# Four early product tiles instead of two at the start of three feed-forward stages

## The chip, the cores and the metric

The kernel runs on one core of a Trainium2 chip. The metric is the device time of one execution in microseconds (us), the median of three runs. TensorE (PE) multiplies matrices, VectorE (DVE), ScalarE (ACT) and GpSimd (POOL) work element by element, and SyncE (SP) issues the DMA transfers. Each engine takes its instructions strictly in the order of its own queue; semaphores tie the queues together. TensorE's clock has two levels here, 2.4 and 1.2 GHz; the profile gives the granted clock as a share of the upper one.

## The reference

Two layers work on 512 tokens (256 context, 256 latent; 1024 features). Each layer is a modulated feed-forward half-step, a token mixer of four parallel head groups, and a second feed-forward half-step:

```
def modulate(x, shift, scale): return x * (1 + scale) + shift
def swiglu(x, wi, wo):
    g, u = jnp.split(x @ wi, 2, axis=-1)
    return (jax.nn.silu(g) * u) @ wo

sc, scc = jax.nn.silu(c), jax.nn.silu(c_ctx)
for l in range(DEPTH):
    mod  = (sc  @ w_mod[l] + b_mod[l]).reshape(b, N_MOD, 1, d)     # latent stream
    modc = (scc @ w_mod[l] + b_mod[l]).reshape(1, N_MOD, 1, d)     # context stream
    h = h + 0.5 * mod[:, 2] * swiglu(modulate(rms_norm(h, ffn1_norm[l]), mod[:, 0], mod[:, 1]), ffn1_wi[l], ffn1_wo[l])
    ...                                        # the same for hc; then the mixer, and the second half-step
```

In the last layer only the latent stream goes on after the mixer. All of it is in float32.

## The kernel before

Features lie on partitions: the state `h` is eight chunks of 128 features by 512 tokens. A product of float32 quality is made of three products in float32r: weight and activation are each split into a high part (a cast) and a low part (the rest), and a tile of 128 output features takes 24 matmuls (`mm3`: eight hi·hi, eight hi·lo, eight lo·hi). `load_split` fetches one weight tile of 128x1024 by DMA (`raw`, three buffers), casts it on ACT (`hi`, two buffers) and subtracts on POOL or DVE in turn (`lo`, two buffers), or on the engine that it is told.

A feed-forward stage (`ffn`) makes 44 tiles `gu` (22 pairs of gate and up), two halves of 11 pairs, each followed by eight output tiles `o`. There are four such stages: the first of layer 0 starts in its own way (`first_tiles`), the later three go through `Normed`. They are called here F2 (second of layer 0, starts at 721 us), F3 (first of layer 1, 1104 us) and F4 (second of layer 1, 1715 us, with 256 token columns instead of 512).

The normalized activation `x` of such a stage needs the root of the mean square over all features, so it can't exist before the last chunk of `h` is there. To bridge this, the first tiles are early: they multiply the weights with `h` times the per-feature scale (`N.pre`, tiles `X`, made by `scale` while the stage before ends), and the factor per token (`R`) and the shift are put in afterwards. `early` therefore also multiplies the same weights with the modulation's shift (`nBs`) into a PSUM bank `bias` (32 small matmuls for a tile), `shift` sums that over partitions (an ACT copy, one matmul, a DVE copy), and `evacuate` multiplies by `R` and adds. Two tiles (NE = 2) are early. In the meantime `finish` makes `R`: sums over partitions on PE (L274), a root by thirteen small DVE instructions (L277 to L284), a broadcast by PE (L287), a copy by ACT (L290). Then `x` makes the eight chunks: chunks 2, 4 and 6 (`POOLX`) begin on POOL (L300) and go on over ACT, the others take DVE (L309), ACT (L311) and DVE (L312). The next two tiles (L497, L498, L501) run chunk by chunk over `x`, and from then on tiles follow by `mm3` (L208, L209, L211).

`mod_groups` computes the remaining modulation columns on DVE beside the first stage and beside F2: each weight row block `wm` (four buffers) is multiplied with silu(c) of one stream, spread over partitions, and summed (L149). The spread vector stands in the two PSUM tiles `c0` and `c1` and is made by 16 float32 matmuls against an identity (L142). `c0` and `c1` also hold the early tiles' `bias`, the sums of `finish`, and in the first stage two product tiles and the sums of `mod_chunk`.

The order within each engine's queue is made by the scheduler of the language when the program is built, from the data dependencies and a few hand-set ones (`behind`, `together`).

Of the kernel before, what the change touches and what calls it, by code (L numbers as in the profile page):

```python
# [20 lines left out]
AF = mybir.ActivationFunctionType  # L21
# [25 lines left out]
def hybrid_block(ctx: ExitStack, tc: tile.TileContext, D, out, dump=lambda *a: None, upto=99):  # L47
# [89 lines left out]
    def mod_groups(l, b0):  # L137

        cb = phase[2]
        for s in range(2):  # L140
            for k in range(NCH):
                mm(cb[s][:, 128 * k:128 * (k + 1)], cs[:, k, s:s + 1].broadcast_to([128, 128]), ident, start=True,  # L142
                   stop=True, skip_group_check=True)
        junk = phase[0].tile([128, 1024], F32, tag="macc", name=nm("macc"), bufs=1)
        for b in range(b0, 72):
            wm = room["wm"]()
            nc.sync.dma_start(out=wm, in_=D["wmod"][l, b])
            for s in range(2):
                stt(out=junk, in0=wm, scalar=1.0, in1=cb[s], op0=ALU.mult, op1=ALU.mult, accum_out=modT[l][:, b, s:s + 1])  # L149
            if b % 8 == 7:  # L150
                m = modT[l][:, b - 7:b + 1, :]
                tt(out=m, in0=m, in1=v3(prm[l][:, P_BM + b - 7:P_BM + b + 1], 8).broadcast_to([128, 8, 2]), op=ALU.add)
            yield
# [59 lines left out]
    class Normed:  # L213
# [52 lines left out]
               op0=ALU.add, op1=ALU.mult)  # L266
            return A, self.late[c][:, 0, :]

        def finish(self, W, PS, tx, ptag):
            self.W, self.tx = W, tx  # L270
            nb = self.n // 128
            ps = PS("n", "ssq")
            for j in range(nb):
# [15 lines left out]
            self.R = kept("R")  # L289
            (nc.vector.tensor_copy if self is norms[0] else nc.scalar.copy)(self.R[:, self.wc], ps[:, self.wc])  # L290
            self.bias = PS(ptag, "bias")

        def x(self, cs_):
            for c in cs_:
# [1 line left out]
                hi, lo = self.W(self.n, s="xh", dt=F32R, tag=self.tx), self.W(self.n, s="xl", dt=F32R, tag=self.tx)  # L296
                wc = self.wc
                A, B = self.AB(c)
                if c in POOLX and not self.late:
                    nc.gpsimd.tensor_tensor(out=t, in0=h[c][:, self.off:T], in1=self.R[:, wc], op=ALU.mult)  # L300
                    for s in self.streams:
                        o = self.sl[s]
                        act(t[:, o], t[:, o], AF.Identity, scale=A[:, s:s + 1], bias=B[:, s:s + 1])
                    nc.scalar.copy(hi[:, wc], t)
                    tt(out=lo[:, wc], in0=t, in1=hi[:, wc].bitcast(F32), op=ALU.subtract)
                else:
                    for s in self.streams:
                        o, b = self.sl[s], B[:, s:s + 1]
                        stt(out=t[:, o], in0=h[c][:, 256 * s:256 * (s + 1)], scalar=A[:, s:s + 1], in1=self.R[:, o],  # L309
                            op0=ALU.mult, op1=ALU.mult)  # L310
                        act(hi[:, o], t[:, o], AF.Identity, bias=b)  # L311
                        i = stt(out=lo[:, o], in0=t[:, o], scalar=b, in1=hi[:, o].bitcast(F32), op0=ALU.add,  # L312
                                op1=ALU.subtract)
                    self.last = i
                self.xs.append((hi, lo))

        def early(self, ps, hi, lo, cc):
# [7 lines left out]
                    behind(i, self.rstd)  # L325
            for k in range(NCH):
                mm(ps[:, cc], lo[:, k, :], self.pre[k][0][:, cc], start=False, stop=(k == NCH - 1))
            b = self.bias[:, 256 * n:256 * n + 128]
            for w in (hi, lo):
                for k in range(NCH):  # L330
                    j = 32 * (k % 4)
# [3 lines left out]

        def shift(self, n):

            b = self.bias[:, 256 * n:256 * n + 128]
            t = self.W(128, s="shift")
            nc.scalar.copy(t, b)  # L340
            b = self.bias[:, 256 * n + 128:256 * n + 130]
            mm(b, t, cst[:, C_SUM:C_SUM + 2], start=True, stop=True, skip_group_check=True)
            sb = small(2, "bias", bufs=4)
            nc.vector.tensor_copy(sb, b)
            return sb
# [5 lines left out]
                op0=ALU.mult, op1=ALU.add)  # L351

    NE = 2
    XC = {2: (range(4), range(4, 8)), 3: (range(2), range(2, 5), range(5, 8))}[NE]
    POOLX = (2, 4, 6)

    def first_tiles(N, wi):
# [68 lines left out]
    def ffn(l, N, wi, wo, m0, streams, hooks={}, nxt=None, fill=None):  # L426
# [10 lines left out]
                next(fill[0], None)  # L437

        if N is not norms[0]:
            N.finish(W, PS, "x", "b")  # L440
        gate = small(16, "gate").rearrange("p (c s) -> p c s", s=2)

        def evacuate(i, gps, ups, bias):
# [20 lines left out]

        ready = []
        head = first_tiles(N, wi) if N is norms[0] else []
        NE = 0 if head else 2
        wt = lambda t: load_split(wi[l, t // 2, t % 2], 1024, nc.gpsimd if t <= NE + 1 else None)
        for half in range(2):
            av = []  # L470
            for i in range(11 * half, 11 * half + 11):
# [3 lines left out]
                for t in range(2 * i + len(gu), 2 * i + 2):  # L475
# [3 lines left out]
                    hi, lo = v3(hi, 8), v3(lo, 8)  # L479
                    if t < NE:  # L480
                        bias.append(N.early(ps, hi, lo, cc))
                        if t:
                            N.x(XC[t - 1])
                        if t == NE - 1:
                            ready.append(wt(NE))
                            N.x(XC[NE - 1])
                    elif t == NE and NE:

                        bias += [None, None]
# [49 lines left out]
    def mixer(l, need_ctx, N, nxt):  # L539
# [179 lines left out]
        for c in range(NE):  # L719
            hi, lo = [v3(a, 8) for a in wt(c)]  # L720
            ps = PS("a", "xbc")
            pend.append((c, ps, N.early(ps, hi, lo, allc)))
            if c:
                N.x(XC[c - 1])
        ready.append(tmw(0))
        N.x(XC[NE - 1])
        xs = N.xs


# [726 lines left out]
def _layout(a):  # L1456
# [5 lines left out]
    cs[:, :, 0] = a["c_ctx"].reshape(8, 128).T  # L1462
    cs[:, :, 1] = a["c"][0].reshape(8, 128).T
    r["cs"] = cs.reshape(128, 256)
    wm = a["w_mod"].reshape(L, 8, 128, 9216)
    r["wmod"] = a["w_mod"].transpose(0, 2, 1).reshape(L, 72, 128, 1024).copy()
    g = wm[0, ..., :2048].reshape(2, 4, 128, 2, 8, 128).transpose(4, 0, 2, 1, 3, 5)
# [81 lines left out]
```

## Time and profile before

| | us |
|---|---|
| median of 3 runs (lowest, highest) | 1928.61 (1928.08, 1929.88) |
| the profiled execution | 1928.47 |
| its span, first to last instruction | 1926.7 |
| TensorE busy (share of span) | 1857.7 (96%) |
| VectorE busy | 1104.3 (57%) |
| ScalarE busy | 797.4 (41%) |
| GpSimd busy | 668.4 (35%) |
| mean granted TensorE clock | 0.975 |

The span is the time from the first to the last instruction of the program; the execution's own time is 1.8 us longer. Busy shares are averages over stages of very different kinds, so what matters is the stretch where the change acts: which engine is idle there and what ended its idle time. Matmuls overlap in the records: the time between two starts is the cost, not the printed duration.

### The profile page before, as it was taken

How to read it: one execution, taken by the hardware profiler on the slowest of the kernel's cores; microseconds unless marked ns; L12 is line 12 of the kernel's file. 1: busy time of each engine (PE TensorE's matmuls, PEld its weight loads, DVE VectorE, ACT ScalarE, POOL GpSimd, SP SyncE). 2: the span in 40 equal slices, each digit the busy share in tenths (PEclk: the TensorE clock that was granted, in tenths of full speed). 3: DMA queues.
4: the chain of work that ended last, by engine and by line, in shares of the span. 5: the costliest groups of instructions: out<-in, count | busy, mean ns of one | idle time of the engine just before them, and what ended most of it. 6: DMA issues, size and time to landing. Idle time of an engine off the chain costs nothing.

```text
span 1926.7 us, 25732 instructions
## 1 busy us (share of the span) xinstructions
PE 1857.7 (96%) x9698; PEld 1500.1 (78%) x9698; DVE 1104.3 (57%) x1952; ACT 797.4 (41%) x1338; POOL 668.4 (35%) x487
## 2 busy tenths in 40 slices
PE   8999999999999998999999989999999998989999
PEld 5788888887765566888888868888888875579999
DVE  5599961368477767999971451121124966674322
ACT  3232233346557544332233442223233575655443
POOL 3233233243323213332333343323323432246564
PEclk8999999999999998999999989999999998989999
DMA  9377842324221012877752322233323332024564
GB/s 361 118 263 241 268 152 89 90 91 132 77 88 34 1 55 93 266 251 254 263 193 81 109 74 91 86 111 99 99 84 100 105 114 66 23 99 162 177 191 128
DMA packets 85244, 259.01 MB, mean 134 GB/s; under 512 B 9312, under 2 KB 15856, under 8 KB 84992
## 3 DMA queue, kind: packets, MB, share of 16 engines
q1 hardware_dynamic: 85056, 257.32, 41.5%
q8 instruction: 76, 1.25, 0.3%
q14 instruction: 48, 0.39, 0.1%
q10 hardware_dynamic: 64, 0.05, 0.0%
HBM read 256.23 MB, written 1.10 MB: 134 GB/s over the span
## 4 chain that ended last, share of the span: by engine, by line
PE 56%; DVE 5%; ACT 1%; issue 1%; POOL 0%; ACTq 0%; DVEq 0%; POOLq 0%
PE gu L208 10%; PE gu L209 10%; PE gu L211 10%; PE o L208 5%; PE o L209 5%; PE o L211 5%; DVE x L309 1%; PE wo L208 1%; PE gu L498 0%; PE gu L501 0%; PE wo L209 0%; PE gu L497 0%; DVE R L250 0%; PE s L129 0%; DVE h L350 0%
## 5 line engine op out<-in xcount | busy, mean ns | idle before, releaser
L201 POOL TENSOR_TENSOR lo<-raw,hi 128x1024 fp32r<-128x1024 f32 (+3 forms) x193 | 425.7, 2206 | 645.6 <-ACT hi L199 288.4
L199 ACT CAST hi<-raw 128x1024 fp32r<-128x1024 f32 (+2 forms) x358 | 340.3, 952 | 661.3 <-PE gu L209 328.7
L208 PE MATMUL gu<-xh,hi 128*128 128x512 f32 (+1 forms) x1264 | 446.1, 362 | 0.0
L209 PE MATMUL gu<-xl,hi 128*128 128x512 f32 (+1 forms) x1264 | 445.8, 362 | 0.0
L149 DVE SCALAR_TENSOR_TENSOR macc<-wm,c 128x1024 f32<-128x1024 f32 x256 | 312.0, 1219 | 7.3 <-PE c L142 0.5
L211 PE MATMUL gu<-xh,lo 128*128 128x512 f32 (+1 forms) x1264 | 278.1, 362 | 0.0
L460 DVE TENSOR_TENSOR a<-gu,sg 128x512 f32<-128x512 f32 (+1 forms) x84 | 52.3, 623 | 383.4 <-PE gu L211 369.6
L208 PEld LDWEIGHTS gu<-xh,hi 128*128 128x128 f32 x1264 | 238.7, 189 | 37.1 <-ACT sg L453 0.3
L209 PEld LDWEIGHTS gu<-xl,hi 128*128 128x128 f32 x1264 | 238.6, 189 | 36.7
L209 PE MATMUL o<-al,hi 128*128 128x512 f32 (+1 forms) x704 | 249.1, 362 | 0.0
L208 PE MATMUL o<-ah,hi 128*128 128x512 f32 (+1 forms) x704 | 248.8, 362 | 0.0
L211 PEld LDWEIGHTS gu<-xh,lo 128*128 128x128 f32 x1264 | 218.5, 189 | 36.8
L462 POOL TENSOR_TENSOR al<-a,ah 128x512 fp32r<-128x512 f32 (+1 forms) x88 | 126.1, 1436 | 299.0 <-ACT ah L461 299.0
L201 DVE TENSOR_TENSOR lo<-raw,hi 128x1024 fp32r<-128x1024 f32 (+2 forms) x165 | 184.4, 1118 | 10.0 <-ACT hi L199 6.9
L350 DVE SCALAR_TENSOR_TENSOR h<-o,gate,h 128x256 f32<-128x256 f32 x112 | 49.7, 479 | 211.4 <-PE o L211 211.4
L211 PE MATMUL o<-ah,lo 128*128 128x512 f32 (+1 forms) x704 | 161.6, 362 | 0.0
L209 PEld LDWEIGHTS o<-al,hi 128*128 128x128 f32 x704 | 132.9, 189 | 20.6
L208 PEld LDWEIGHTS o<-ah,hi 128*128 128x128 f32 x704 | 132.7, 189 | 20.6
L211 PEld LDWEIGHTS o<-ah,lo 128*128 128x128 f32 x704 | 122.5, 189 | 20.6
L461 ACT CAST ah<-a 128x512 fp32r<-128x512 f32 (+1 forms) x88 | 49.9, 568 | 116.4 <-DVE a L460 116.3
L678 POOL TENSOR_SCALAR_AFFINE_SELECT E<-bc 128x256 f32<-128x256 f32 (+1 forms) x96 | 37.2, 424 | 85.4 <-PE y L131 33.5
L453 ACT ACTIVATE sg<-gu 128x512 f32<-128x512 f32 (+1 forms) x84 | 45.6, 544 | 46.1 <-PE gu L211 45.7
(428 smaller groups left out, 2556.0 us busy)
## 6 DMA issues: line engine op xcount, KB each, us to landing
raw<-in_wi_dram SPq DMA_DIRECT2D x170, 512.0 KB, 3.6
wm<-in_wmod_dram SPq DMA_DIRECT2D x136, 512.0 KB, 4.4
raw<-in_wo_dram SPq DMA_DIRECT2D x64, 384.0 KB, 3.1
raw<-in_wo_dram SPq DMA_DIRECT2D x64, 320.0 KB, 3.0
raw<-in_win_dram SPq DMA_DIRECT2D x36, 512.0 KB, 3.5
raw<-in_wout_dram SPq DMA_DIRECT2D x16, 512.0 KB, 3.6
bc<-br SPq DMA_DIRECT2D x20, 256.0 KB, 4.6
X<-in_wmod_dram SPq DMA_DIRECT2D x16, 256.0 KB, 6.8
```

Source lines behind the costliest of these rows:

```text
L149: stt(out=junk, in0=wm, scalar=1.0, in1=cb[s], op0=ALU.mult, op1=ALU.mult, accum_out=modT[l][:, b, s:s + 1])
L199: nc.scalar.copy(hi, raw)
L201: (eng or (nc.gpsimd if nsplit[0] % 2 else nc.vector)).tensor_tensor(out=lo, in0=raw, in1=hi.bitcast(F32), op=ALU.subtract)
L208: mm(ps[:, cols], whi(k), xs[k][0][:, cols], start=(first and k == 0), stop=False)
L209: mm(ps[:, cols], whi(k), xs[k][1][:, cols], start=False, stop=False)
L211: mm(ps[:, cols], wlo(k), xs[k][0][:, cols], start=False, stop=(last and k == n - 1))
L350: stt(out=h[d][:, sc], in0=ps[:, 256 * s - off:256 * (s + 1) - off], scalar=gate[:, d, s:s + 1], in1=h[d][:, sc], op0=ALU.mult, op1=ALU.add)
L453: act(sg, gps[:, cc], AF.Silu)
L460: tt(out=a, in0=ups[:, cc], in1=sg, op=ALU.mult)
L461: nc.scalar.copy(ah, a)
L462: nc.gpsimd.tensor_tensor(out=al, in0=a, in1=ah.bitcast(F32), op=ALU.subtract)
L678: nc.gpsimd.affine_select(out=o, in_=src[:, r], pattern=[[sg, r.stop - r.start]], compare_op=ALU.is_ge, fill=fill, base=sg * (r.start - 12 ...
```

## The change

In F2, F3 and F4 four tiles are early instead of two. `x` is made in three portions between them (chunks 0 and 1; 2 to 4; 5 to 7), all eight chunks on the DVE path, none on POOL. The low parts of early tiles 2 and 3 are made on DVE, of tiles 0, 1, 4 and 5 on POOL. The four bias results fill one PSUM half bank, their sums stand in another (`stag`). The mixer keeps two early tiles and its POOL chunks. In `mod_groups` the spread vector is no longer made by matmuls: two DMAs copy the raw conditioning row from DRAM to all partitions (`crow`, into two of the `wm` buffers), and ACT writes its silu into the PSUM tiles, four instructions of 128x512.

```
@@ mod_groups
         for s in range(2):
-            for k in range(NCH):
-                mm(cb[s][:, 128 * k:128 * (k + 1)], cs[:, k, s:s + 1].broadcast_to([128, 128]), ident, start=True,
-                   stop=True, skip_group_check=True)
+            t = room["wm"]()
+            nc.sync.dma_start(out=t, in_=D["crow"][s:s + 1, :].broadcast_to([128, 1024]))
+            for i in range(2):
+                act(cb[s][:, 512 * i:512 * (i + 1)], t[:, 512 * i:512 * (i + 1)], AF.Silu)
@@ Normed.finish
-        def finish(self, W, PS, tx, ptag):
-            self.W, self.tx = W, tx
+        def finish(self, W, PS, tx, ptag, stag=None):
+            self.W, self.tx, self.pool = W, tx, stag is None
...
             self.bias = PS(ptag, "bias")
+            if stag:
+                sums = PS(stag, "sums")
+                self.bias = [(self.bias[:, 128 * n:128 * (n + 1)], sums[:, 2 * n:2 * n + 2]) for n in range(4)]
+            else:
+                self.bias = [(self.bias[:, 256 * n:256 * n + 128], self.bias[:, 256 * n + 128:256 * n + 130])
+                             for n in range(2)]
@@ Normed.x
-                if c in POOLX and not self.late:
+                if c in POOLX and self.pool and not self.late:
@@ the portions of x, by the number of early tiles
-    XC = {2: (range(4), range(4, 8)), 3: (range(2), range(2, 5), range(5, 8))}[NE]
+    XC = {2: ((), range(4), range(4, 8)), 4: ((), range(2), range(2, 5), range(5, 8))}
@@ ffn
-            N.finish(W, PS, "x", "b")
+            N.finish(W, PS, "x", "b", "m")
...
-        NE = 0 if head else 2
-        wt = lambda t: load_split(wi[l, t // 2, t % 2], 1024, nc.gpsimd if t <= NE + 1 else None)
+        NE = 0 if head else 4
+        wt = lambda t: load_split(wi[l, t // 2, t % 2], 1024,
+                                  None if t > NE + 1 else nc.vector if 1 < t < NE else nc.gpsimd)
...
                     if t < NE:
                         bias.append(N.early(ps, hi, lo, cc))
-                        if t:
-                            N.x(XC[t - 1])
+                        N.x(XC[NE][t])
                         if t == NE - 1:
                             ready.append(wt(NE))
-                            N.x(XC[NE - 1])
```

The built programs show where the instructions went. TensorE's queue at the start of F3, before: the last bias matmuls of the second early tile, then the first tile that needs `x` (`xh`, `xl`).

```order
L332 MATMUL c_1695_8940<-hi_9017,nBs_8522 32x128 x8
L332 MATMUL c_1695_8940<-lo_9018,nBs_8522 32x128 x8
L497 MATMUL gu_9159<-xh_9063,hi_9098 128x512
L498 MATMUL gu_9159<-xl_9064,hi_9098 128x512
L497 MATMUL gu_9159<-xh_9072,hi_9098 128x512
```

The same place now (the changed file's lines are eight or nine higher): a third and a fourth early tile (`X`), and their bias matmuls, stand ahead of the first `xh`.

```order
L340 MATMUL c_1703_8973<-hi_9050,nBs_8555 32x128 x8
L340 MATMUL c_1703_8973<-lo_9051,nBs_8555 32x128 x8
L330 MATMUL gu_9135<-X_8607,hi_9137 128x512
...
L331 MATMUL gu_9135<-X_8959,hi_9137 128x512
L330 MATMUL gu_9209<-X_8607,hi_9211 128x512
...
L340 MATMUL c_1703_8973<-hi_9211,nBs_8555 32x128 x8
L340 MATMUL c_1703_8973<-lo_9212,nBs_8555 32x128 x8
L505 MATMUL gu_9311<-xh_9096,hi_9284 128x512
```

So 48 matmuls of 512 columns and 32 + 32 small ones moved in between. VectorE's queue at the same place, from the first chunk of `x` on, before:

```order
L309 SCALAR_TENSOR_TENSOR x_9062<-h_70,nA_8519,R_8965 128x256 x2
L309 SCALAR_TENSOR_TENSOR x_9071<-h_71,nA_8519,R_8965 128x256 x2
L309 SCALAR_TENSOR_TENSOR x_9088<-h_73,nA_8519,R_8965 128x256 x2
L309 SCALAR_TENSOR_TENSOR x_9111<-h_75,nA_8519,R_8965 128x256 x2
L312 SCALAR_TENSOR_TENSOR xl_9064<-x_9062,modT_95,xh_9063 128x256 x2
L312 SCALAR_TENSOR_TENSOR xl_9073<-x_9071,modT_95,xh_9072 128x256 x2
L305 TENSOR_TENSOR xl_9082<-x_9080,xh_9081 128x512
```

And now:

```order
L317 SCALAR_TENSOR_TENSOR x_9095<-h_70,nA_8552,R_8998 128x256 x2
L317 SCALAR_TENSOR_TENSOR x_9104<-h_71,nA_8552,R_8998 128x256 x2
L320 SCALAR_TENSOR_TENSOR xl_9097<-x_9095,modT_95,xh_9096 128x256 x2
L320 SCALAR_TENSOR_TENSOR xl_9106<-x_9104,modT_95,xh_9105 128x256 x2
L202 TENSOR_TENSOR lo_9138<-raw_9136,hi_9137 128x1024
L458 TENSOR_TENSOR sg_9123<-gu_9001,R_8998 128x512
L464 TENSOR_TENSOR a_9124<-gu_9048,R_8998 128x512
L317 SCALAR_TENSOR_TENSOR x_9182<-h_72,nA_8552,R_8998 128x256 x2
L317 SCALAR_TENSOR_TENSOR x_9191<-h_73,nA_8552,R_8998 128x256 x2
L202 TENSOR_TENSOR lo_9212<-raw_9210,hi_9211 128x1024
```

The low parts of two weight tiles and two multiplications of finished products by `R` now stand between the chunks of `x`, and chunks 2, 4 and 6 are VectorE's too. The third place is in the first stage, VectorE's queue at 66 us, where the last chunk of `x` is made. Before:

```order
L265 TENSOR_SCALAR nA_123_602<-mod_119_596,prm_68 128x2
L309 SCALAR_TENSOR_TENSOR x_599<-h_77,nA_123_602,R_217 128x256 x2
L312 SCALAR_TENSOR_TENSOR xl_601<-x_599,mod_119_596,xh_600 128x256 x2
L149 SCALAR_TENSOR_TENSOR macc_812,modT_94<-wm_813,c_1_102 128x1024
L201 TENSOR_TENSOR lo_753<-raw_751,hi_752 128x1024
```

Now:

```order
L266 TENSOR_SCALAR nA_123_602<-mod_119_596,prm_68 128x2
L317 SCALAR_TENSOR_TENSOR x_599<-h_77,nA_123_602,R_217 128x256 x2
L150 SCALAR_TENSOR_TENSOR macc_804,modT_94<-wm_805,c_1_102 128x1024
L320 SCALAR_TENSOR_TENSOR xl_601<-x_599,mod_119_596,xh_600 128x256 x2
L202 TENSOR_TENSOR lo_753<-raw_751,hi_752 128x1024
```

The first product of `mod_groups` slipped ahead of the last `xl`; on ScalarE the two silu instructions that it reads stand just ahead of that chunk's `xh`.

## Rows read from the trace of the kernel before

**Rows 1.** Busy time by window: window, its length, PE, PEld, DVE, ACT, POOL, clock, DMA, GB/s.
```profile
813.00:861.00 48.00, 48.00 (x214) 39.74 (x213) 46.75 (x74) 14.77 (x18) 18.54 (x10) 1.00 0.82 258
1104.00:1141.00 37.00, 30.70 (x185) 24.24 (x184) 25.80 (x51) 17.92 (x35) 14.19 (x7) 0.86 0.18 57
1720.50:1733.50 13.00, 9.38 (x39) 8.62 (x40) 10.13 (x22) 5.93 (x10) 7.32 (x5) 0.50 0.26 83
```
**Rows 2.** Timeline of PE, start of F3: start, duration, instruction, [idle before <-what ended it].
```profile
1117.91 0.64 PE L332 MATMUL c<-hi,nBs 128*32 128x128 f32 x16
...
1119.25 0.62 PE L332 MATMUL c<-lo,nBs 128*32 128x128 f32 x16
1121.86 0.50 PE L497 MATMUL gu<-xh,hi 128*128 128x512 f32 x1 [1.99 <-ACT hi L199]
...
1128.53 0.80 PE L498 MATMUL gu<-xl,hi 128*128 128x512 f32 x1 [4.08 <-DVE xl L312]
...
1140.57 0.39 PE L208 MATMUL gu<-xh,hi 128*128 128x512 f32 x1
...
1151.45 0.39 PE L208 MATMUL gu<-xh,hi 128*128 128x512 f32 x1
```
**Rows 3.** Timeline of DVE and POOL, start of F3.
```profile
1114.06 5.35 DVE L309 SCALAR_TENSOR_TENSOR x<-h,nA,R 128x256 f32<-128x256 f32 x8 [1.95 <-ACT R L290]
1119.34 1.66 DVE L312 SCALAR_TENSOR_TENSOR xl<-x,modT,xh 128x256 fp32r<-128x256 f32 x4
...
1122.60 5.09 DVE L309 SCALAR_TENSOR_TENSOR x<-h,nA,R 128x256 f32<-128x256 f32 x2
...
1122.09 5.32 POOL L201 TENSOR_TENSOR lo<-raw,hi 128x1024 fp32r<-128x1024 f32 x2
```
**Rows 4.** Timeline of PE and DVE, start of F2.
```profile
730.26 1.91 PE L142 MATMUL c<-cst,cs 128*128 128x128 f32 x8
...
737.94 0.48 PE L322 MATMUL gu<-X,hi 128*128 128x512 f32 x1
...
744.12 0.62 PE L332 MATMUL c<-lo,nBs 128*32 128x128 f32 x16
...
777.96 0.39 PE L208 MATMUL gu<-xh,hi 128*128 128x512 f32 x1
...
729.98 0.68 DVE L250 TENSOR_TENSOR R<-R,sq 128x512 f32<-128x512 f32 x1
```
**Rows 5.** Timeline of POOL, DVE and PE, start of F4.
```profile
1722.63 4.67 POOL L201 TENSOR_TENSOR lo<-raw,hi 128x1024 fp32r<-128x1024 f32 x2 [2.88 <-ACT hi L199]
...
1725.06 2.27 DVE L279 TENSOR_SCALAR ry<-ry 128x2 int32<-128x2 int32 x1
...
1729.14 1.22 PE L287 MATMUL c<-cst,ry 128*128 128x128 f32 x4 [3.62 <-DVE ry L284]
...
1744.64 0.28 PE L208 MATMUL gu<-xh,hi 128*128 128x256 f32 x1
...
1750.40 0.28 PE L208 MATMUL gu<-xh,hi 128*128 128x256 f32 x1
```
**Rows 6.** Timeline of PE, DVE and ACT in the first stage.
```profile
34.90 0.61 PE L178 MATMUL c<-cst,macc 128*128 128x2 f32 x4 [1.98 <-DVE macc L175]
...
66.54 2.05 PE L142 MATMUL c<-cst,cs 128*128 128x128 f32 x16 [0.44 <-DVE mod L183]
68.35 1.18 PE L394 MATMUL gu<-xh,hi 128*128 128x512 f32 x4
...
83.63 1.95 PE L142 MATMUL c<-cst,cs 128*128 128x128 f32 x16
...
68.65 1.21 DVE L149 SCALAR_TENSOR_TENSOR macc<-wm,c 128x1024 f32<-128x1024 f32 x1
...
67.31 0.91 ACT L311 ACTIVATE xh<-x,mod 128x256 fp32r<-128x256 f32 x2 [8.99 <-DVE x L309]
72.94 0.60 ACT L453 ACTIVATE sg<-c 128x512 f32<-128x512 f32 x1
```

More of the change, by code (lines that the diff above doesn't have):

```diff
@@ L327, in early @@
                 mm(ps[:, cc], lo[:, k, :], self.pre[k][0][:, cc], start=False, stop=(k == NCH - 1))
-            b = self.bias[:, 256 * n:256 * n + 128]
+            b = self.bias[n][0]
             for w in (hi, lo):
@@ L336, in shift @@
         def shift(self, n):
-            b = self.bias[:, 256 * n:256 * n + 128]
+            b, sums = self.bias[n]
             t = self.W(128, s="shift")
             nc.scalar.copy(t, b)
-            b = self.bias[:, 256 * n + 128:256 * n + 130]
+            b = sums
             mm(b, t, cst[:, C_SUM:C_SUM + 2], start=True, stop=True, skip_group_check=True)
@@ L722, in mixer @@
             pend.append((c, ps, N.early(ps, hi, lo, allc)))
-            if c:
-                N.x(XC[c - 1])
+            N.x(XC[NE][c])
         ready.append(tmw(0))
-        N.x(XC[NE - 1])
+        N.x(XC[NE][NE])
         xs = N.xs
@@ L1464, in _layout @@
     r["cs"] = cs.reshape(128, 256)
+    r["crow"] = np.stack([a["c_ctx"].reshape(-1), a["c"].reshape(-1)])
     wm = a["w_mod"].reshape(L, 8, 128, 9216)
```

## The prediction

> **What bounds the kernel now.** The first view to read is the busy time by window [rows 1]. In the 48 us from 813 TensorE is busy for all 48.00 at clock 1.00, with VectorE busy 46.75 beside it. There nothing can be won but by taking matmuls away. In the 37 us in which F3 begins it is busy 30.70 and its clock is 0.86 in the mean; in 13 us at the start of F4 it is busy 9.38 at clock 0.50. So a stage's start is where time is lost, and since TensorE then runs without a gap to the stage's end, a microsecond saved at the start arrives at the end.
>
> The second view is TensorE's timeline at F3's start [rows 2]. The early tiles' bias matmuls begin at 1117.91 in four groups and end at about 1119.7 (the fourth starts at 1119.25; a third of the distance between first and fourth, 0.45, is one group's cost). Then come 1.99 us of idle time for the cast of the next weight tile on ScalarE, and 4.08 us for an `xl` of VectorE. Four tiles are through at 1140.57, six at 1151.45: a steady tile costs (1151.45 - 1140.57) / 2 = 5.44.
>
> The third view says why `xl` is late [rows 3]. Two half-chunk instructions of L309 took 5.09 us while POOL's two weight splits took 5.32, and the eight before them 5.35. The L312 instructions, of the same size, took 1.66 / 4 = 0.42 each. R is there at 1114.06.
>
> **The change part by part. F3.** Two more tiles that need neither R nor `x` now stand between 1119.7 and the first `xh`. Up to the sixth tile's end TensorE has, from 1119.7 on: tiles 2 and 3, 10.9; their bias, two times two groups of 0.45, 1.8; the four `shift` sums, which I price as four float32 matmuls of L142's kind (1.91 / 8 = 0.24 each [rows 4]), 1.0; tiles 4 and 5, 10.9. That is 1144.3 against 1151.45: **-7.2**. It holds only if no wait comes back and the clock stays up.
>
> What must be in time is VectorE's chain. TensorE takes the last `xl` in the chunk-by-chunk pass of tile 4: 1119.7 + 10.9 + 1.8 + 1.0 + two thirds of a tile (16 of 24 matmuls), 3.6, is 1137.0, that is 22.9 after R. The chain holds 32 half-chunk instructions at 0.42 (13.4), the low parts of tiles 2 and 3 (the nearest 128x1024 instruction took 1.21 [rows 6]: 2.4) and three 128x512 products at 0.68 [rows 4] (2.0): 17.8. To this comes a wait of some 2.1 for the cast of tile 2, whose buffer comes free with the bias matmuls of `hi` at about 1118.4 and is filled by ScalarE in about 1.1 us (an estimate: 512 columns took 0.60 [rows 6]): VectorE would have made two chunks by 1117.4 and stands until 1119.5. In all 20 us, a slack of 2.9. Behind the waiting low part stand the products by R and chunks 2 to 7, and for these wait ScalarE's `xh` and TensorE. The cause of the 4.08 goes in part: POOL has no chunks any more, and of the splits in this stretch only those of tiles 4 and 5.
>
> Those splits are where a rule speaks against the change. By the rows, a POOL split and VectorE's instructions beside it stretch to the same length (5.32 and 5.09 [rows 3]). The Trainium skill, "SBUF — State Buffer", section "SBUF: two separate sides", says that a GpSimd instruction and a VectorE instruction with two SBUF inputs share a port pair as an exclusive lock, and that the loser stands until the other has finished. By that rule the splits of tiles 4 and 5 still stop VectorE; the trace agrees as far as those rows go. Worked out from rows: one split is 2.34 to 2.66 [rows 3, 5]; if one falls into the chain, it takes 2.4 of the 2.9 and nothing happens; if both do, VectorE is 1.9 late. The second case is rival A.
>
> **F2.** Six tiles were through at 777.96 [rows 4]. The first group of L142 (16 records, eight of them in 1.91 at half clock) stands in TensorE's queue between the last products with `X` and the sums for R, from 730.26 on. VectorE's last sum of squares, which the sums wait for, is ready at 729.98 + 0.68 = 730.7, so taking the group out brings the chain forward. I take 1.9, the first eight records; the bounds are 0, if the root's chain of small VectorE instructions sets 737.94 alone, and 3.8, if all 16 count at that price. The broadcast is done by 736.0 instead of 737.94. From there to the end of the bias TensorE needs 744.12 + 0.45 - 737.94 = 6.6, hence 742.6, and then the same 24.6 as in F3: 767.2, **-10.8**. This contains a second group of L142 that stood behind tile 3, 1.8.
>
> **F4.** POOL's splits of tiles 2 and 3 ran from 1722.63 for 4.67, and in them VectorE's L279, an instruction of two columns, took 2.27 [rows 5]. TensorE waited 3.62 for that chain until 1729.14. The two splits are VectorE's now and stand behind the chain, so L279 gives back 2.1 and its neighbour, also inside the split, about 1 (an estimate): 1726.1. A tile of 256 columns is (1750.40 - 1744.64) / 2 = 2.88. From 1726.1 there are the broadcast, 0.9, the rest of tile 1 (20 of 24 matmuls, 2.4 at full and 4.8 at half clock; I take 3.5), four tiles' bias 3.6, `shift` 1.0 and tiles 2 to 5, 11.5: 1746.6, **-3.8**. Bounds: -2.5 (the rest of tile 1 at half clock throughout) and -4.9 (at full clock).
>
> **The first stage.** L142 leaves twice. The second group stood between steady tiles: 1.8 (the distance from 66.54 to 68.35 for the same 16 records [rows 6]). The first stood in a place where TensorE has nothing else to do, before the last chunk of `x`. ScalarE now makes two silu of 0.60 each ahead of that chunk's `xh`, and VectorE a product of 1.21 ahead of its `xl`. If all of that counted, 2.4 would be lost against the 1.8 that go; ScalarE had stood idle for 8.99 before that `xh`, so its part should fit in, and of VectorE's 1.21 I count half, 0.6. I take -1.8 + 0.6 = **-1.2**, bounds -1.8 and +0.6. The gap at 66.5 us grows from 0.44 to about 2.4. The nearest row is a gap of 1.98 at 34.90 in the same stage [rows 6], the other is F3's 1.99, behind which the clock did fall [rows 2]. If it falls here, I price it as in F3, 0.14 x 37 = 5.2 [rows 1].
>
> The two row transfers stand in SP's queue ahead of the first weight blocks and take two of their four buffers until the silu is done. I cost this at nothing, since VectorE's products begin only at 68.65; without that cover it is one product's time, 1.2, on VectorE, which TensorE doesn't feel. The mixers keep their two early tiles, and cost nothing.
>
> **Sum.** -7.2 - 10.8 - 3.8 - 1.2 = -23.0. For small waits at four new places I add 0.5 each (the smallest gap shown is 0.44): -21.0. The profiled execution took 1928.47 (the span 1926.7 and 1.8 around it), 0.14 below the median of the runs: 1928.47 - 21.0 = 1907.5, so **1907**, own range 1902 to 1913.
>
> **The rivals.** A: VectorE's chain comes late. The ground for it is the slack of 2.9 against two splits of 2.4, and that the chain's 0.42 was read where POOL was quiet; against it, that POOL splits those tiles late, when most chunks are made. A wait of 1.9 in F2 and F3 costs 3.8, so 1911; if the clock falls behind each, 5.2 twice more, 1921.
>
> B: F2's gain is given back, because VectorE paces the stage there. It is busy 46.75 of 48 [rows 1] with the products of `mod_groups`, and the change doesn't remove one of them; if TensorE comes 10.8 earlier and VectorE can't follow, that is lost: 1918. Against it: TensorE had no gap in that stretch, so VectorE has kept up with it at a later start and only its products' end moves into the stage.
>
> C, the slower side: chunks on VectorE stay as slow as now. Ten L309 took 5.35 + 5.09, 1.04 each [rows 3]. If POOL isn't the cause, sixteen of them cost 16.7 and not 6.7, and the chain takes 30, 7.1 past the limit of 22.9 from which this decides. F2 and F3 then lose 7.1 + 5.2 each, against gains of 10.8 and 7.2, and F4 half as much, 6.2 against 3.8: +1.5, +5.1 and +2.4, with -1.2 of the first stage +7.8, 1936. Against it stand L312's 0.42 and L279's 2.27, which show VectorE stopped by POOL and not by its own work.
>
> D: the clock falls at 66 us: 1907.5 + 5.2 = 1912.7, which is inside the forecast's own range.
>
> **How the numbers follow.** The forecast with D has 0.64, A 0.20, B 0.10, C 0.05, and 0.01 is left for more than all of the sum. The range 1902 to 1919 holds the forecast, B and most of A. 0.2% is 3.9 us, about what a measurement of this kernel tells from no change: 1924.8 to 1932.5. Faster are the forecast, B and A but for its worst, a loss of both kinds in all three stages: 0.92; that worst part lies within, 0.03; C is slower, 0.05.
>
> **What would show it.** In F3 no wait of 1.99 and 4.08, the clock 1.00 from 1119 on, `xl` of the last chunk made no later than TensorE's 17 us behind the early bias; in F4 a wait below 1 us where 3.62 was; L142 gone; F2's sixth tile at 46 us behind the stage's start and not at 57. The forecast is wrong if an `xl` stops TensorE in tile 4 or 5, if VectorE's chunks take 1 us a half without POOL beside them, or if the stages' later tiles have gaps.

## The result and the profile after

The changed kernel took 1905.33 us (median of four runs, 1903.74 to 1908.03) against 1929.24 for the kernel before (four runs too): a ratio of 0.9878, with a 95% interval of 0.9861 to 0.9895, or 24 us less. The forecast was 1907. In a second series, with the kernel before measured again beside it, the same program took 1907.96, a ratio of 0.9902 (0.9886 to 0.9918), by which it is 19 us less; the forecast's 21 lies between the two. The profiled execution took 1903.74, its span is 1902.0, and the mean granted clock rose from 0.975 to 0.986.

The busy time by window of the changed kernel, same columns as in [rows 1]; F3 and F4 start 11 and 20 us earlier now, and the windows with them.

```profile
802.00:850.00 48.00, 48.00 (x213) 39.77 (x212) 44.63 (x73) 14.77 (x18) 17.85 (x10) 1.00 0.76 246
1093.00:1130.00 37.00, 36.77 (x277) 29.20 (x277) 27.82 (x64) 17.30 (x36) 9.86 (x4) 1.00 0.25 76
1700.50:1713.50 13.00, 12.63 (x125) 11.55 (x126) 11.67 (x26) 6.70 (x13) 4.94 (x2) 0.74 0.35 105
60.00:72.00 12.00, 9.42 (x48) 7.10 (x48) 3.90 (x10) 2.90 (x5) 0.00 (x0) 0.87 0.16 55
```

The last of these windows in the kernel before:

```profile
60.00:72.00 12.00, 11.56 (x72) 9.14 (x71) 3.90 (x10) 2.83 (x5) 0.80 (x1) 1.00 0.05 12
```

At F3's start TensorE is busy 36.77 of 37 us where it was busy 30.70, and its clock is 1.00 instead of 0.86. At F4's start it is 12.63 of 13 where it was 9.38, with the clock at 0.74. The steady stretch is full as before. The last window is the first stage's, where the changed kernel is worse: TensorE is busy 9.42 instead of 11.56 (some 1.8 of which were L142's matmuls), and its clock is 0.87 instead of 1.00.

TensorE's timeline of the changed kernel at F3's start (lines of the changed file are eight to nine higher: L340 is L332 of before, L505 and L506 are L497 and L498).

```profile
1100.85 1.16 PE L289 MATMUL c<-cst,ry 128*128 128x128 f32 x8 [0.23 <-DVE ry L286]
...
1107.94 0.62 PE L340 MATMUL c<-lo,nBs 128*32 128x128 f32 x16
1108.49 0.50 PE L330 MATMUL gu<-X,hi 128*128 128x512 f32 x1
...
1122.96 0.50 PE L505 MATMUL gu<-xh,hi 128*128 128x512 f32 x1
1123.29 0.39 PE L506 MATMUL gu<-xl,hi 128*128 128x512 f32 x1
...
1134.48 0.39 PE L209 MATMUL gu<-xh,hi 128*128 128x512 f32 x1
```

From the broadcast (L289) on no row carries a wait: the waits of 1.99 and 4.08 of [rows 2] are gone. Two early tiles and their bias take 1108.49 to 1122.96, 14.5 us, and the two tiles after them 11.5. VectorE and POOL beside it:

```profile
1102.66 1.67 DVE L317 SCALAR_TENSOR_TENSOR x<-h,nA,R 128x256 f32<-128x256 f32 x4 [1.87 <-ACT R L292]
...
1115.15 2.46 DVE L317 SCALAR_TENSOR_TENSOR x<-h,nA,R 128x256 f32<-128x256 f32 x6
...
1117.99 2.67 POOL L202 TENSOR_TENSOR lo<-raw,hi 128x1024 fp32r<-128x1024 f32 x1 [22.26 <-ACT hi L200]
...
1118.39 2.96 DVE L317 SCALAR_TENSOR_TENSOR x<-h,nA,R 128x256 f32<-128x256 f32 x2
...
1124.52 1.26 DVE L320 SCALAR_TENSOR_TENSOR xl<-x,modT,xh 128x256 fp32r<-128x256 f32 x3
```

Without POOL beside them, four half chunks take 1.67 and six 2.46, 0.41 to 0.42 each, the value that the forecast took from another instruction. Beside POOL's split of tile 4 the last two take 2.96. The last `xl` is ready at 1125.8, 23.1 us after the chunks' beginning at 1102.66; the forecast had set 20 for the work and 22.9 as the limit. TensorE takes it at 1126.5, since its own work had also become longer. So the chain just fits.

In F2 it doesn't quite. TensorE's rows first, then VectorE's and POOL's, and last TensorE's wait for X in the kernel before:

```profile
724.89 0.80 PE L331 MATMUL gu<-X,hi 128*128 128x512 f32 x1 [3.31 <-DVE X L258]
...
731.61 1.16 PE L289 MATMUL c<-cst,ry 128*128 128x128 f32 x8 [0.23 <-DVE ry L286]
...
758.49 0.50 PE L506 MATMUL gu<-xl,hi 128*128 128x512 f32 x1 [1.06 <-DVE xl L320]
...
766.64 0.39 PE L209 MATMUL gu<-xh,hi 128*128 128x512 f32 x1
...
721.55 2.35 POOL L202 TENSOR_TENSOR lo<-raw,hi 128x1024 fp32r<-128x1024 f32 x1 [5.39 <-ACT hi L200]
721.90 2.54 DVE L251 TENSOR_TENSOR R<-R,sq 128x512 f32<-128x512 f32 x1
...
753.21 5.23 DVE L320 SCALAR_TENSOR_TENSOR xl<-x,modT,xh 128x256 fp32r<-128x256 f32 x5
...
754.01 1.62 POOL L471 TENSOR_TENSOR al<-a,ah 128x512 fp32r<-128x512 f32 x1 [2.60 <-ACT ah L470]
755.59 2.57 POOL L202 TENSOR_TENSOR lo<-raw,hi 128x1024 fp32r<-128x1024 f32 x1
```

```profile
727.54 0.79 PE L323 MATMUL gu<-X,hi 128*128 128x512 f32 x1 [3.30 <-DVE X L257]
```

Five `xl` took 5.23 beside two POOL instructions (2.1 without), and TensorE waited 1.06 for the last. The wait of 3.31 for X, which the change was not to touch (3.30 before), is in part POOL's too: a sum of squares took 2.54 where it takes 0.68 [rows 4], beside the split of tile 1. Six tiles are through at 766.64, 11.3 us earlier than before [rows 4], of which 2.65 were there before the stage's X (724.89 against 727.54).

F4 and the first stage, TensorE:

```profile
1705.90 1.22 PE L289 MATMUL c<-cst,ry 128*128 128x128 f32 x4 [0.29 <-DVE ry L286]
...
1725.90 0.28 PE L209 MATMUL gu<-xh,hi 128*128 128x256 f32 x1
...
68.49 1.70 PE L403 MATMUL gu<-xh,hi 128*128 128x512 f32 x4 [2.58 <-ACT xh L319]
...
74.30 0.39 PE L209 MATMUL gu<-xh,hi 128*128 128x512 f32 x1
```

The wait for the root in F4 fell from 3.62 [rows 5] to 0.29, and six tiles are through at 1725.90. In the first stage the wait at 66 us is 2.58, four matmuls behind it take 1.70 instead of 1.18 [rows 6], and the next tile begins 5.81 us after the start of those four; before, these were 68.35 and 72.62, 4.27:

```profile
72.62 0.50 PE L208 MATMUL gu<-xh,hi 128*128 128x512 f32 x1
```

To say where the 24.7 us of the two spans went, both were cut at rows that stand in every trace: TensorE's wait for ScalarE near 476 in the first mixer, for POOL near 690 at its end, the broadcast of F3, the wait for ScalarE near 1510 where the second mixer begins, and the wait for VectorE near 1653 towards its end. Lengths are differences of the rows' starts, so the end of a mixer stands in the column of the stage behind it. The runs of the experiments stand beside them, one profile of each.

| us | first stage | mixer 1 | F2 | F3 | mixer 2 | F4 | span |
|---|---|---|---|---|---|---|---|
| before | 476.2 | 215.5 | 420.5 | 415.1 | 146.0 | 253.5 | 1926.7 |
| changed | 475.9 | 213.1 | 411.9 | 409.4 | 143.1 | 248.7 | 1902.0 |
| changed, again | 476.1 | 213.2 | 414.3 | 409.4 | 145.1 | 249.7 | 1907.8 |
| early tiles alone | 476.4 | 216.3 | 414.1 | 409.4 | 145.0 | 248.7 | 1909.9 |
| silu alone | 476.3 | 216.9 | 415.6 | 415.8 | 143.8 | 252.8 | 1921.1 |
| chunks on POOL | 476.5 | 216.7 | 414.1 | 410.5 | 141.9 | 250.9 | 1910.5 |
| splits 2, 3 on POOL | 474.9 | 215.7 | 410.9 | 409.8 | 141.7 | 253.0 | 1906.0 |
| splits 0 to 3 on VectorE | 476.0 | 215.7 | 412.0 | 409.4 | 141.7 | 251.1 | 1905.9 |
| all splits on VectorE | 477.4 | 217.3 | 412.0 | 409.4 | 141.7 | 247.9 | 1905.7 |
| silu late | 474.8 | 211.7 | 414.2 | 409.4 | 142.0 | 248.4 | 1900.5 |
| filled gap | 478.5 | 215.5 | 410.5 | 409.4 | 144.8 | 249.7 | 1908.3 |
| all fixes | 477.9 | 211.7 | 407.8 | 409.4 | 142.8 | 250.1 | 1899.6 |
| fixes, one pin less | 475.0 | 215.7 | 410.0 | 409.4 | 144.9 | 250.9 | 1905.8 |

Between the first two rows the stages give 19.4 (0.3, 8.7, 5.7 and 4.8, each rounded) and the mixers, whose matmuls the change leaves as they were, 5.3.

### The profile page after: what moved, and what is told of

Same layout as the page of the kernel before. It is cut to its first block, busy times and chain, and to the rows that moved or that the text cites. A ratio compares the mean times of both kernels' runs of the same rounds, so it can differ in the third digit from the quotient of the medians.

```text
span 1902.0 us, 26039 instructions
## 1 busy us (share of the span) xinstructions
PE 1845.6 (97%) x9838; PEld 1491.3 (78%) x9838; DVE 1112.8 (59%) x1990; ACT 797.2 (42%) x1345; POOL 650.4 (34%) x475
## 4 chain that ended last, share of the span: by engine, by line
PE 57%; DVE 4%; ACT 1%; issue 1%; DMA 0%; POOL 0%; ACTq 0%; POOLq 0%; DVEq 0%; SPq 0%
PE gu L210 9%; PE gu L209 9%; PE gu L212 9%; PE o L212 5%; PE o L209 5%; PE o L210 5%; PE gu L330 1%; PE gu L331 1%; PE gu L335 1%; PE c L340 1%; PE wo L209 1%; PE gu L509 1%; ACT E L611 0%; PE gu L506 0%; PE gu L505 0%
## 5 line engine op out<-in xcount | busy, mean ns | idle before, releaser
L202 POOL TENSOR_TENSOR lo<-raw,hi 128x1024 fp32r<-128x1024 f32 (+3 forms) x190 | 419.6, 2209 | 671.0 <-ACT hi L200 296.7
L209 PE MATMUL gu<-xh,hi 128*128 128x512 f32 (+1 forms) x1216 | 429.4, 362 | 0.0
L210 PE MATMUL gu<-xl,hi 128*128 128x512 f32 (+1 forms) x1216 | 429.4, 362 | 0.0
L212 PE MATMUL gu<-xh,lo 128*128 128x512 f32 (+1 forms) x1216 | 267.9, 362 | 0.0
L210 PEld LDWEIGHTS gu<-xl,hi 128*128 128x128 f32 x1216 | 229.6, 189 | 35.6
L209 PEld LDWEIGHTS gu<-xh,hi 128*128 128x128 f32 x1216 | 229.5, 189 | 35.5
L212 PEld LDWEIGHTS gu<-xh,lo 128*128 128x128 f32 x1216 | 210.4, 189 | 35.5
L202 DVE TENSOR_TENSOR lo<-raw,hi 128x1024 fp32r<-128x1024 f32 (+1 forms) x168 | 185.8, 1106 | 16.1 <-ACT hi L200 13.1
```

Source lines behind the costliest of these rows:

```text
L202: (eng or (nc.gpsimd if nsplit[0] % 2 else nc.vector)).tensor_tensor(out=lo, in0=raw, in1=hi.bitcast(F32), op=ALU.subtract)
L209: mm(ps[:, cols], whi(k), xs[k][0][:, cols], start=(first and k == 0), stop=False)
L210: mm(ps[:, cols], whi(k), xs[k][1][:, cols], start=False, stop=False)
L212: mm(ps[:, cols], wlo(k), xs[k][0][:, cols], start=False, stop=(last and k == n - 1))
```

## The experiments

### The two halves of the change alone

The early tiles without the new spread vector: in `mod_groups`

```
-            t = room["wm"]()
-            nc.sync.dma_start(out=t, in_=D["crow"][s:s + 1, :].broadcast_to([128, 1024]))
-            for i in range(2):
-                act(cb[s][:, 512 * i:512 * (i + 1)], t[:, 512 * i:512 * (i + 1)], AF.Silu)
+            for k in range(NCH):
+                mm(cb[s][:, 128 * k:128 * (k + 1)], cs[:, k, s:s + 1].broadcast_to([128, 128]), ident, start=True,
+                   stop=True, skip_group_check=True)
```

> Four early tiles, but the spread vector still made by 16 + 16 small matmuls (L142). Theory: the parts add up. F2 keeps the two groups of L142, 1.9 and 1.8 us, and the first stage is as before, where the trace of the changed kernel shows a gain of only 0.15: 1905.3 + 3.7 = 1909 us, and the clock is 1.00 from 60 to 72 us. Rival: the matmuls only filled waits, and the time is 1905, that of the whole change.

It took 1914.14 us, 0.9922 of before (0.9908 to 0.9937), 15 us less. F3 is 409.4 long as in the whole change, so its gain is the early tiles' alone. F2 is 2.3 longer than in the changed kernel's first profile but the same as in its second. The median was 5 above what was expected, and the profile's stages were not: its two mixers took 361.3 together, 5.1 more than the changed kernel's first profile. The clock from 60 to 72 us was 1.00, as expected.

The same edit the other way round, applied to the kernel before:

> The rows spread by DMA and the silu, with two early tiles as before. Theory: -3.7 us from F2 and nothing from the first stage, where the longer gap at 66 us lets the clock fall and eats the 1.8: about 1925.5. Rival 1, the forecast's term: the first stage gives 1.2 as well, 1924.3. Rival 2: hidden anyway, 1929.

It took 1923.20, 0.9968 (0.9956 to 0.9981), 6.2 less, 2 more than expected. F2 gained 4.9 and the first stage nothing (476.3 against 476.2), which speaks against the forecast's -1.2 there. By the ratios the halves give 15.0 + 6.2 = 21.2, the whole change 23.5 and 18.9 in its two series: the totals add up within what the series differ by. Stage by stage they don't: in F2 the halves give 4.9 + 6.4 = 11.3, the whole change 8.7 and 6.2. A part of the 4.9 may be the clock and not L142's own time: in the 16 us from the end of the wait for X on it was 0.91 here and 0.81 before.

### Which engine makes the chunks

`self.pool` was set to True, so that chunks 2, 4 and 6 begin on POOL, with four early tiles.

```
-            self.W, self.tx, self.pool = W, tx, stag is None
+            self.W, self.tx, self.pool = W, tx, True
```

> The whole change, but chunks 2, 4 and 6 of x begin on POOL as before. Theory: POOL locks VectorE, so x is late again: waits for xl of 2 to 4 us in F2 and F3, with the clock falling behind them, 1911 to 1921. Rival: the two more early tiles (14.5 us of TensorE work in F3) cover the old lateness of 4.08 + 1.99 whatever engine makes the chunks: 1905 within 2.

1911.17, 0.9903 (0.9890 to 0.9917). F3 is 1.1 longer, F2 is as in the changed kernel's second profile, and in each of them one wait for `xl` of 0.75 stands. The time is the lowest that the theory named, but the theory's waits of 2 to 4 us did not come: by the waits the rival is nearer. Most of F3's gain is the cover, not the engine: 4.6 of 5.7 are left. That the run lies 6 above the first series is, by its profile, in the first mixer (some 3.5), which the edit doesn't touch, in F2 (2.2), where the half clock behind X lasted longer (clock 0.70 in the 16 us from the wait's end on, against 0.91), and in F4 (2.2).

### The splits of tiles 2 and 3 on POOL

```
-                                  None if t > NE + 1 else nc.vector if 1 < t < NE else nc.gpsimd)
+                                  None if t > NE + 1 else nc.gpsimd)
```

> The whole change, but the low parts of early tiles 2 and 3 are POOL's as well. Theory: in F4 POOL's splits stop the root chain on VectorE again, a wait of about 3.6 before the broadcast instead of 0.29, and the half clock lasts longer: 1908.6 to 1910. In F2 and F3 VectorE is free of 2.4 us but stands behind two more splits of 2.4 us each. Rival: VectorE's chain is shorter and F2's last wait of 1.06 goes as well: 1904 or less.

1910.72, 0.9902 (0.9888 to 0.9915), just above the theory's 1908.6 to 1910. VectorE, POOL and TensorE of this run at F4's start:

```profile
1702.45 4.67 POOL L202 TENSOR_TENSOR lo<-raw,hi 128x1024 fp32r<-128x1024 f32 x2 [2.88 <-ACT hi L200]
1703.26 1.58 DVE L280 TENSOR_SCALAR ry<-rv 128x2 int32<-128x2 int32 x1
1704.88 2.27 DVE L281 TENSOR_SCALAR ry<-ry 128x2 int32<-128x2 int32 x1
...
1708.96 1.22 PE L289 MATMUL c<-cst,ry 128*128 128x128 f32 x4 [3.81 <-DVE ry L286]
```

These are the rows of the kernel before again [rows 5], to the hundredth in the split's and L281's durations, and F4 is 253.0 long, 0.5 less than before the change. So with four early tiles F4's gain hangs on this one line; the line with two early tiles was not run. In F2 there is no wait for `xl`, as the rival said, and the stage is 1.0 shorter. That isn't the edit's doing for certain: of the eleven profiles with four early tiles only the changed kernel's two (1.06 and 1.07) and the one with chunks on POOL (0.75) have that wait, and three of the others (early tiles alone, silu late, filled gap) leave the splits where the change put them.

The same run shows the first stage from another side:

```profile
68.81 1.19 PE L403 MATMUL gu<-xh,hi 128*128 128x512 f32 x4 [2.58 <-ACT xh L319]
...
73.16 0.50 PE L209 MATMUL gu<-xh,hi 128*128 128x512 f32 x1
```

The wait is 2.58 as in the changed kernel, yet the four matmuls took 1.19 and the clock from 60 to 72 us was 1.00; the next tile begins 4.35 after their start, and the stretch to 476 is 1.0 shorter.

### The splits of tiles 0 and 1, and of all six, on VectorE

The first run has `nc.vector if t < NE else nc.gpsimd` in that line, the second `nc.vector` for all six.

> The whole change, and the low parts of early tiles 0 and 1 on VectorE as well (POOL keeps those of tiles 4 and 5). Theory: the wait of 3.31 us for X at F2's start, and the waits of 1.16 and 1.67 at F4's, are POOL's splits of tiles 0 and 1 stopping VectorE (three L258 took 3.41 us beside a split of 2.90, an L251 2.54 beside one of 2.35). On VectorE each costs about 1.2 and no lock: F2's wait falls to about 1 to 1.5 with less half clock behind it, F4's to under 1: 2 to 5 us less than the whole change, 1901 to 1903. Rival: VectorE is full there (10.00 of 10 us) and is the limit itself: the same or later X, 1905 to 1908.

> All six splits at a stage's start on VectorE. Theory: besides the gain at tiles 0 and 1, the wait of 1.06 for the last xl in F2 goes, since POOL's split of tile 5 (2.57 us) beside five L320 (5.23 us) was its cause and the same work costs VectorE 1.2: 1900 to 1902. Rival: two more splits on VectorE, 2.4 us, stand ahead of the last chunks and the wait becomes 1 to 2 us and appears in F3 too.

1910.22, 0.9909 (0.9892 to 0.9926), and 1906.39, 0.9887 (0.9870 to 0.9904), where 1901 to 1903 and 1900 to 1902 were expected: both missed. The wait for X in F2 fell to 1.75 in both, but another took its place. TensorE in the first of the two runs:

```profile
728.10 0.50 PE L331 MATMUL gu<-X,hi 128*128 128x512 f32 x1 [1.75 <-DVE X L258]
...
734.47 2.07 PE L289 MATMUL c<-cst,ry 128*128 128x128 f32 x8 [2.43 <-DVE ry L286]
```

The built order had moved the sums for R (L276) behind the eight products with the low weights, which had covered the root's chain: 3.31 + 0.23 became 1.75 + 2.43. F2 is 412.0 long in both, as in the changed kernel's first profile. In F4 the same order left a wait of 2.63 ahead of the broadcast in the first run and of 0.59 in the second, and the stage is 2.4 longer and 0.8 shorter. The second run shows no wait for `xl`, as its theory said, but neither does the first, where POOL still splits tiles 4 and 5; so it doesn't show that the split of tile 5 was the cause.

### The silu and the first modulation product behind the last chunk

```
+                if l == 0:
+                    behind(si, norms[0].lastx)     # silu: behind the last xh on ScalarE
...
+                if l == 0 and b == b0:
+                    behind(pi, norms[0].last)      # first product: behind the last xl on VectorE
```

> The whole change, with the silu of the spread rows behind the last chunk's xh on ScalarE, and the first product of the modulation behind its xl on VectorE. Theory: at 68 us the wait of 2.58 shrinks to about 2.0 and the xl stands no longer behind a product of 1.2: 0.5 to 1.2 less at the seventh tile (74.30 in the trace of the change), 2.5 if the clock then stays up. Rival: the wait is the chunk's own chain (modulation, x, xh), nothing changes but the order.

1903.82, 0.9878 (0.9862 to 0.9895), the same as the changed kernel's first series. TensorE in this run:

```profile
68.66 1.20 PE L407 MATMUL gu<-xh,hi 128*128 128x512 f32 x4 [2.16 <-ACT xh L323]
...
72.94 0.50 PE L213 MATMUL gu<-xh,hi 128*128 128x512 f32 x1
```

The wait is 0.4 shorter, the clock from 60 to 72 us is 1.00, and the next tile begins 4.28 after these matmuls, as before the change (4.27). From the last sums of `mod_chunk` (66.00) to this seventh tile it is 6.94, 1.9 less than in the changed kernel, where 2.5 was expected if the clock stays up. The stretch to 476 is 1.1 shorter; the run with POOL's splits, without this edit, had 1.0 there, so the wait's 0.4 is what the edit itself shows. The two later runs with the same edit (all fixes, and one pin less) show too that the clock is not settled by it: behind the same 2.16 the four matmuls took 2.00 and 2.07, at half clock.

### Matmuls in the gap

Nine 128x128 matmuls without a use, into a free part of the bank that `mod_chunk` sums in, behind its last sums.

```
+        if c == NCH - 1:
+            for _ in range(9):
+                mm(ps[:, 384:512], ident, ident, start=True, stop=True, skip_group_check=True)
```

> The whole change, with nine small matmuls that compute nothing needed, in the wait at 66 us (0.24 us each, 2.1 in all). Theory: the clock falls because TensorE stands there; with the wait filled it stays 1.00 from 60 to 72 us (0.87 in the trace of the change), and the seventh tile starts 1.5 us earlier, at 72.8, although TensorE does more. Rival: the fall has another cause, or the last xl is what ends last (VectorE's product ahead of it): then nothing is gained, or a wait for xl of about 1 us appears.

1911.23, 0.9912 (0.9898 to 0.9926). The edit missed its own purpose:

```profile
66.19 2.25 PE L184 MATMUL c<-cst 128*128 128x128 f32 x18
68.49 0.34 DVE L188 TENSOR_SCALAR mod<-c,prm 128x2 f32<-128x2 f32 x2 [6.35 <-PE c L184]
...
71.03 1.22 PE L407 MATMUL gu<-xh,hi 128*128 128x512 f32 x2 [2.58 <-ACT xh L323]
```

VectorE reads the sums of that bank only after the matmuls that were put behind them, so the whole chunk came 2.2 later and the wait of 2.58 stood behind the filling, not in it. Whether a filled wait would keep the clock up stays open: with L142's matmuls there the clock was 1.00 (the kernel before [rows 6], and the early tiles alone), but so it was behind the empty 2.58 of the run with POOL's splits.

### The same program again, and the fixes together

The changed kernel without an edit:

> The changed kernel once more, nothing edited, for the part of its gain that the stages don't explain: in the first pair of traces the two token mixers, whose instructions are the same, were 4.0 and 2.9 us shorter. Theory: that is chance, TensorE's clock behind the mixers' waits of 2 to 3 us, and the stretch from the wait near 476 to the one near 691 (213.1 us there, 217.1 before) will come out elsewhere between 213 and 218, with the stages' own lengths the same within 1 us (F3's 409.4). Rival: it is this program's own, and 213 comes again.

1907.96, 0.9902. F3 is the same to 0.01 us. Mixer 1 came out at 213.2 again, so the theory of chance has no support there (the expectation's 217.1 for the kernel before is wrong: it is 215.5 by the rows of the table, and the difference 2.4 and not 4.0). Mixer 2 is 2.0 longer, F2 2.5 and F4 1.0, without another instruction; so the stages' lengths were not the same within 1 us, as the theory had them. F2's difference is the clock behind the wait of 3.31:

```profile
724.00:740.00 16.00, 14.87 (x120) 11.83 (x121) 10.46 (x32) 5.66 (x10) 0.00 (x0) 0.89 0.44 165
```

```profile
724.00:740.00 16.00, 14.82 (x53) 12.15 (x53) 9.96 (x31) 3.78 (x8) 0.18 (x1) 0.68 0.48 165
```

The first is the first profile of the changed kernel, the second the one again: the same window, TensorE busy for as long (14.87 and 14.82), clock 0.89 and 0.68.

All fixes: the late silu, six splits on VectorE, and

```
+                if n == 0 and k == 0 and self.pool is False:
+                    behind(i, self.ssq)            # the low products behind the sums for R
...
+        if after:
+            behind(i, after)                       # the split of tile 1 behind the last X
```

> The whole change with four edits: silu and first modulation product behind the last chunk in the first stage, all six weight splits at a stage's start on VectorE, the second tile's split behind the last X, and the sums for R ahead of the eight products with the low weights. Theory: the waits of 3.31 in F2 and 1.67 in F4 shrink to about 1 each, the wait for the root stays at 0.3 since the eight products cover it again, and no xl is late: 3 to 5 us less than the whole change, near 1901. Rival: VectorE, with six splits of 1.2, ends the chunks too late in F3, and 1 to 3 us come back as waits for xl.

> As the run with all fixes, but the second tile's split isn't tied behind the last X. Theory: the split stays ahead of the last X on VectorE in F2 and F4 and the wait there is 1.75, as in the runs with the splits on VectorE: 1 to 1.5 us more than with all fixes. Rival: the wait has another cause and is the same in both.

With all fixes 1903.67 (1897.78 to 1906.54), 0.9878 (0.9858 to 0.9899); without the pin of tile 1's split 1907.89, 0.9898 (0.9881 to 0.9915). TensorE with all fixes at F2's start:

```profile
724.75 0.50 PE L337 MATMUL gu<-X,hi 128*128 128x512 f32 x1 [0.62 <-DVE X L264]
725.84 1.02 PE L282 MATMUL c<-cst,R 128*128 128x1 f32 x8 [0.36 <-DVE R L257]
...
729.53 1.16 PE L295 MATMUL c<-cst,ry 128*128 128x128 f32 x8 [0.46 <-DVE ry L292]
```

The waits of 3.31 and 0.23 are 0.62, 0.36 and 0.46, no half clock follows, and F2 is 407.8, the shortest of all thirteen. In F4 nothing is gained: TensorE waits 1.42 there for the last sum of squares, which the scheduler put behind the pinned split, and the stage is 1.4 longer than with the change alone. By its span this is the fastest profile (1899.6); by the medians it can't be told from the changed kernel's first series, and it is 4 us below the second, with intervals of the ratios that overlap; near 1901 was expected. Without the pin the wait for X in F2 is 1.76, as expected, F2 is 2.2 longer than with it, and F4 is no shorter for it (250.9).

## Why the prediction was right, step by step

**Where the time is.** Right. The gains lie at the stages' starts and reach the end: F3's length from its broadcast into the second mixer is 409.4 in nine of the eleven profiles with four early tiles (410.5 and 409.8 in the two where POOL has more to do), and 415.1 and 415.8 in the two with two early tiles.

**F3, -7.2.** The mechanism was right and the term 1.5 too large: -5.7 in both profiles. The waits are gone and the clock is 1.00, as set out. What was mis-sized is TensorE's own work: two early tiles with bias take 14.5 and not 13.7 (10.9 + 1.8 + 1.0), tiles 4 and 5 11.5 and not 10.9. The steady tile's 5.44 was taken for tiles that are made otherwise, and this makes 1.4 of the 1.5.

**VectorE's chain.** Right in its price of 0.42 a half chunk, and in that the splits of tiles 4 and 5 would stop it: the chain took 23.1 where 20 were set. In F3 TensorE's longer work hid that; in F2 rival A came true with 1.06 us where it had 1.9, without a fall of the clock. By the prediction's own sign, an `xl` that stops TensorE in tile 4 or 5, this is a fault of the overlap, if a small one. Rival C fell: six half chunks took 2.46 without POOL beside them, 0.41 each and not 1.04. Rival B, that VectorE paces F2, fell too: TensorE is busy 48.00 of the 48 us from 802, and F2 kept its gain to the end.

**F2, -10.8.** The mechanism was right, the size again too large: -8.7 in the first profile and -6.2 in the second, which differ by the clock behind the wait for X. In the first profile the tiles' own length is 1.4 more than set, as in F3, and the pass with the wait for `xl` another 1.4 (754 to 767: 12.9 us against F3's 11.5); the way from X to the broadcast gave 2.9 where 1.9 was set. Taking only L142 out gave 4.9, the early tiles alone 6.4.

**F4, -3.8.** Right: -4.8 and -3.8, of which 3.3 are the root's wait (3.62 to 0.29); in the run with POOL's splits it is back, with 3.81.

**The first stage, -1.2.** Wrong: -0.3 and 0.0 in the two profiles, +0.2 with the silu alone. The second group of L142 gave its 1.8. The step that failed is the one that put half of VectorE's product, 0.6, and no fall of the clock into the sum: from the last sums of `mod_chunk` (65.60 before, 65.41 now) to the seventh tile it is 7.02 before and 8.89 in the changed kernel, 1.9 more. The wait grew to 2.58 and the clock fell, in both profiles of this program. Rival D was right in kind and its price of 5.2 too high: 5.81 - 4.27 = 1.5. It is no sure price either, since behind the same 2.58 the run with POOL's splits kept the clock at 1.00.

**The sum.** The four terms were -23.0, the stages gave -19.4 and -15.7. The difference, 3.6 and 7.3, is more than the allowance of 2.0 for small waits: mostly the tiles' own length and the clock behind X. That the total still came out at -24 in the first series is the mixers' 5.3 (3.2 in the second profile), which the forecast had at nothing; so its closeness to 1907 is in part luck. The second mixer and F2 move by 2 to 3 us between two profiles of one program. The first mixer's 213.1 came again in the same program and lay between 211.7 and 217.3 in the others, and with it goes the clock from 476 to 492, behind a wait of 2.7 to 2.9 us with the same instructions in front: the four profiles at 1.00 have 211.7 to 213.2, the five at 0.89 215.5 to 215.7, the four at 0.79 216.3 to 217.3. Why one program keeps to the one and another to the other is not settled.

## What to carry to other kernels

Where a steady stage is full, look only at its start, and cover what is late there with work that needs nothing of it: the cover counts more than which engine does the late work. Where two engines stop one another, put the long instructions of the one where the other has no chain running, and look at the order that the build makes of it, since a wait that goes can come back one place further. And a tile that is made in another way is priced from a row of its own kind.

## What the runs showed of the hardware

The half clock behind a wait is not a fixed price. Behind the same 2.16 us of wait four matmuls took 1.20, 2.00 and 2.07 us in three kernels, and behind the same 2.58 1.70 in the changed kernel and 1.19 in the run with POOL's splits; at the same wait of 3.3 the clock from 724 to 740 us was 0.89 and 0.68 in two profiles of one program. One program came to 0.9878 and to 0.9902 of before in two series, 5 us apart by these ratios (2.6 by its own medians), so an edit of 1 to 3 us is read here from the traces, stage by stage, and not from the medians.

POOL and VectorE stop one another for whole instructions: L281 of 128x2 took 2.27 us beside a POOL split and 0.17 in the changed kernel's F4, where no split stood beside it. The Trainium skill, "SBUF — State Buffer", section "SBUF: two separate sides", calls the ports that the two engines share an exclusive lock that one holds for its whole instruction, and the trace agrees with that. Who gets it is not to be foreseen from these timelines: five `xl` took 2.06 us in the run with the filled gap, where POOL's subtraction began 0.8 after the first of them and itself took 2.41, and 5.23 in the changed kernel, where it began 0.8 after as well and took 1.62. In the first case TensorE did not wait in tile 4, in the second 1.06 us. From the changed kernel's F4, and from F2 of the run with the filled gap:

```profile
1703.91 0.17 DVE L281 TENSOR_SCALAR ry<-ry 128x2 int32<-128x2 int32 x1
...
758.19 2.06 DVE L324 SCALAR_TENSOR_TENSOR xl<-x,modT,xh 128x256 fp32r<-128x256 f32 x5
...
759.00 2.41 POOL L475 TENSOR_TENSOR al<-a,ah 128x512 fp32r<-128x512 f32 x1 [2.60 <-ACT ah L474]
```
